# Average pooling over 512 MiB on one core: 4 MiB stores over two tiles, a side buffer for a tile's last sums, and a first load in one piece

## The chip, the cores and the metric

The kernel runs on one core of a Trainium2 chip. The metric is the device time of one execution in microseconds (us). The kernel before takes 1575.64 us, the median of 3 runs between 1575.11 and 1575.70.

The engines that matter here are VectorE (DVE), which adds; ScalarE (ACT), which multiplies and also issues stores; and SyncE (SP), which issues loads and a few stores. Their transfers are carried out by 16 DMA engines, which all three share.

## The reference

```python
x = np.random.randn(64, 256, 8192).astype(np.float32)   # kernel_size = stride = 4
out_len = (length - kernel_size) // stride + 1          # 2048
for i in range(out_len):
    start = i * stride
    output[:, :, i] = np.mean(x[:, :, start : start + kernel_size], axis=2)
```

Each output is the mean of four neighbouring numbers. 536.87 MB are read, 134.22 MB are written, and there is no reuse of anything.

## The kernel before

The input is taken as 16384 rows of 8192 floats, the output as 16384 rows of 2048. A tile is 256 rows: two whole rows (`_R = 2`) for each of the 128 partitions, 64 KiB of input per partition and 8 MiB in all, and 16 KiB of output per partition, 2 MiB in all. There are 64 tiles. A tile is one contiguous piece of HBM, in which a partition's 64 KiB follow directly on the 64 KiB of the partition before (`xg`, line 43).

In SBUF there are two input buffers (`xin`, 2 x 64 KiB per partition) and four output buffers (`res`, 4 x 16 KiB per partition). The order of the work is written out by hand, engine by engine, with semaphores, and no scheduler moves it. Each engine runs a loop over groups of four tiles (`U = _NOUT = 4`), the last group outside it.

- SP (`load`, lines 67 to 74) waits until the sums of the tile two before are done (`s_dve`), and then loads the next tile into that tile's buffer. All loads go through SP's queue. In the last group the last tile is loaded as two halves of one row per partition, each 4 MiB.
- The first tile is loaded by two DMAs (lines 114 and 115): partitions 0 to 15 (`_S = 16`) with the semaphore `s_first`, and partitions 16 to 127 with `s_in[0]`. DVE waits for the first of them at line 130, and for the second in `add_up`.
- DVE (`add_up`, lines 92 to 104) waits until the output buffer has been stored (`s_out`) and the tile has landed (`s_in`). It then adds neighbours twice (`pairs`, line 88): first 16384 floats per partition to 8192, written in place over the front half of the input buffer, then 8192 to 4096, written to the output buffer. Only the second sum gives the input buffer back (`s_dve`).
- ACT (lines 141 to 156) waits for the sums, multiplies the output buffer by 0.25 in place, waits for that, and issues the store of the tile (line 150), 2 MiB. The first tile's store is issued after the second tile's sums (line 142).
- At the end SP issues the stores of tiles 61 and 62 and of the first row of tile 63 behind the last loads (lines 125 to 127), and, after the critical section, the store of the last row, 1 MiB (line 162).

Of the kernel before, what the change touches and what calls it, by code (L numbers as in the profile page):

```python
# [1 line left out]

# [4 lines left out]

_R = 2  # L10

_NIN = 2
_NOUT = 4

_S = 16


@with_exitstack
def kernel(
    ctx: ExitStack,  # L20
    tc: tile.TileContext,
    x: bass.AP,
    kernel_size: bass.AP,
    stride: bass.AP,
    out: bass.AP,
):
    nc = tc.nc
    K = int(kernel_size)
    assert K == int(stride) == 4
    P = nc.NUM_PARTITIONS  # L30
    dt = x.dtype
    inv_k = 1.0 / float(K)

    xf = x.flatten_outer_dims()
    of = out.flatten_outer_dims()
    rows, L = xf.shape
    OL = of.shape[1]
    R = _R
    T, OT = R * L, R * OL
    assert OL * K == L and rows % (P * R * _NOUT) == 0  # L40
    NT = rows // (P * R)

    xg = xf.rearrange("(t p r) m -> p t (r m)", p=P, r=R)
    og = of.rearrange("(t p r) m -> p t (r m)", p=P, r=R)

    pool = ctx.enter_context(tc.tile_pool(name="buf", bufs=1))
    xin = pool.tile([P, _NIN * T], dt)
    res = pool.tile([P, _NOUT * OT], dt)

    s_in = [tc.alloc_semaphore(f"s_in{b}") for b in range(_NIN)]
    s_out = [tc.alloc_semaphore(f"s_out{b}") for b in range(_NOUT)]
    s_dve = tc.alloc_semaphore("s_dve")
    s_act = tc.alloc_semaphore("s_act")
    s_half = tc.alloc_semaphore("s_half")
    s_last = tc.alloc_semaphore("s_last")
    s_first = tc.alloc_semaphore("s_first")

    with tc.tile_critical():  # L60

        U = _NOUT
        E = NT // U - 1

        def load(h, u, r0=0, r1=R, wait=True):
            b = u % _NIN
            if wait:
                nc.sync.wait_ge(s_dve, h * U + (u - _NIN + 1))  # L70
            nc.sync.dma_start(  # L71
                out=xin[:, b * T + r0 * L : b * T + r1 * L],
                in_=xg[:, h * U + u, r0 * L : r1 * L],
            ).then_inc(s_last if r0 > 0 else s_in[b], 16)

        def obuf(u, r0=0, r1=R):
            return res[:, u * OT + r0 * OL : u * OT + r1 * OL]

        def store(eng, h, u, r1=R):

            eng.wait_ge(s_act, h * U + (u + (1 if r1 == R else r1)))
            eng.dma_start(
                out=og[:, h * U + u, : r1 * OL], in_=obuf(u, 0, r1)
            ).then_inc(s_out[u], 16)

        def pairs(out, src):
            v = src.rearrange("p (m k) -> p m k", k=2)
            return nc.vector.tensor_tensor(  # L88
                out=out, in0=v[:, :, 0], in1=v[:, :, 1], op=mybir.AluOpType.add
            )  # L90

        def add_up(h, u, r0=0, r1=R):

            b = u % _NIN
            if r0 > 0:
                nc.vector.wait_ge(s_last, 16)
            else:
                nc.vector.wait_ge(s_out[u], h * 16)
                nc.vector.wait_ge(s_in[b], h * (U // _NIN * 16) + (u // _NIN + 1) * 16)  # L99
            src = xin[:, b * T + r0 * L : b * T + r1 * L]  # L100
            half = src[:, : (r1 - r0) * L // 2]
            pairs(half, src).then_inc(s_half, 1)
            nc.vector.wait_ge(s_half, h * U + (u + 1 + (r0 > 0)))
            pairs(obuf(u, r0, r1), half).then_inc(s_dve, 1)

        def scale(h, u, r0=0, r1=R):
            nc.scalar.wait_ge(s_dve, h * U + (u + 1 + (r0 > 0)))
            o = obuf(u, r0, r1)
            nc.scalar.mul(o, o, inv_k).then_inc(s_act, 1)  # L109

        for p0, p1, sem in ((0, _S, s_first), (_S, P, s_in[0])):
            nc.sync.dma_start(out=xin[p0:p1, :T], in_=xg[p0:p1, 0, :]).then_inc(sem, 16)  # L115
        for u in range(1, _NIN):
            load(0, u, wait=False)
        with nc.sync.Fori(0, E) as h:
            for u in range(_NIN, U + _NIN):
                load(h, u)  # L120
        for u in range(_NIN, U - 1):
            load(E, u)
        for r in range(R):
            load(E, U - 1, r, r + 1, wait=r == 0)
        for u in range(1, U - 1):
            store(nc.sync, E, u)
        store(nc.sync, E, U - 1, R - 1)


        nc.vector.wait_ge(s_first, 16)  # L130
        with nc.vector.Fori(0, E) as h:
            for u in range(U):
                add_up(h, u)
        for u in range(U - 1):
            add_up(E, u)
        for r in range(R):
            add_up(E, U - 1, r, r + 1)

        scale(0, 0)
        nc.scalar.wait_ge(s_dve, 2)
        store(nc.scalar, 0, 0)
        with nc.scalar.Fori(0, E) as h:
            for u in range(1, U + 1):
                v = u % U
                nc.scalar.wait_ge(s_dve, h * U + (u + 1))
                nc.scalar.mul(obuf(v), obuf(v), inv_k).then_inc(s_act, 1)  # L148
                nc.scalar.wait_ge(s_act, h * U + (u + 1))
                nc.scalar.dma_start(out=og[:, h * U + u, :], in_=obuf(v)).then_inc(  # L150
                    s_out[v], 16
                )
        scale(E, 1)
        scale(E, 2)
        scale(E, 3, 0, 1)
        scale(E, 3, 1, 2)

        nc.sync.wait_ge(s_out[0], E * 16 + 16)

    nc.sync.dma_start(
        out=og[:, NT - 1, (R - 1) * OL :], in_=res[:, _NOUT * OT - OL :]
    )


# [1 line left out]
_INS = ['x', 'kernel_size', 'stride']  # L168
_OUTS = [((64, 256, 2048), 'float32')]

_NUMBERS = {'kernel_size': 4, 'stride': 4}


# [26 lines left out]
```

## Time and profile before

| what | value |
|---|---|
| median of 3 runs | 1575.64 us |
| the profiled execution's own time | 1575.64 us |
| its span, first to last instruction | 1573.9 us |
| DVE busy | 839.8 us, 130 instructions |
| ACT busy | 232.9 us, 66 instructions |
| bytes moved by DMA | 671.10 MB, mean 426 GB/s |
| SP's queue (q1) | 543.17 MB, 81.0% of the 16 engines' span |
| ACT's queue (q10) | 127.93 MB, 19.0% |
| DVE's wait for loads | 723.1 us in 65 waits |
| a store of 2 MiB on ACT's queue | 52.8 us from issue to landing, median |

The span leaves out 1.7 us of the profiled execution's own time. The page cuts the span into 40 slices of 39.35 us; for each it gives the busy share of each engine in tenths, of the DMA engines taken together, and the GB/s that they moved. The trace also has a record for every DMA packet (one contiguous run of bytes on one DMA engine) with its start, its duration and its size. A load's packet here is the 64 KiB of one partition, a store's packet the 16 KiB of one partition. The busy share of the DMA engines counts the time that packets took, so a packet that is slow counts as busy too.

### The profile page before, as it was taken

The numbers are of one execution on the slowest core, as the hardware profiler recorded it, in microseconds if no ns is written. First come the engines' busy times: TensorE is split into PE (matmuls) and PEld (weight loads), VectorE is DVE, ScalarE is ACT, GpSimd is POOL, SyncE is SP. The second block draws the span as 40 slices with busy tenths as digits, with TensorE's granted clock in tenths as the row PEclk, the third lists the DMA queues.
The fourth block names the chain that finished last, engine by engine and source line by source line (L and its number), as shares of the span: only waits on it lengthen the run. The fifth ranks groups of instructions, "written<-read, shape, count | busy, mean of one in ns | idle before, by whom it ended". The sixth has DMA issues, their size and how long they took to land.

```text
span 1573.9 us, 977 instructions
## 1 busy us (share of the span) xinstructions
DVE 839.8 (53%) x130; ACT 232.9 (15%) x66; POOL 0.2 (0%) x4
## 2 busy tenths in 40 slices
DVE  0654654645546546456465464564654645646546
ACT  0111111011011111110110111101101111011011
POOL 0000000000000000000000000000000000000000
DMA  9999999999999999999999999999999999999999
GB/s 213 413 428 433 433 433 433 434 433 444 422 436 433 436 434 434 436 434 434 435 433 433 432 434 433 431 437 433 433 433 433 433 433 429 437 433 433 433 428 396
DMA packets 18736, 671.10 MB, mean 426 GB/s; under 512 B 2096, under 2 KB 2096, under 8 KB 2096
## 3 DMA queue, kind: packets, MB, share of 16 engines
q1 hardware_dynamic: 9952, 543.17, 81.0%
q10 hardware_dynamic: 8784, 127.93, 19.0%
HBM read 536.87 MB, written 134.22 MB: 426 GB/s over the span
## 4 chain that ended last, share of the span: by engine, by line
DMA 71%; DVE 27%; another core or an unknown queue 0%; issue 0%; SPq 0%; ACT 0%; DVEq 0%
DMA xin<-in_x_dram 71%; DVE xin L88 18%; DVE res L88 9%; SPq L71 0%; ACT res L109 0%; DVEq L99 0%; SPq L115 0%; SPq L195 0%; SPq L60 0%
## 5 line engine op out<-in xcount | busy, mean ns | idle before, releaser
L88 DVE TENSOR_TENSOR xin<-xin 128x8192 f32<-128x8192 f32 (+1 forms) x65 | 556.5, 8561 | 723.1 <-DMA xin<-in_x_dram 723.1
L148 ACT ACTIVATE res<-res 128x4096 f32<-128x4096 f32 x60 | 217.0, 3616 | 1224.7 <-DVE res L88 1224.7
L88 DVE TENSOR_TENSOR res<-xin 128x4096 f32<-128x4096 f32 (+1 forms) x65 | 283.4, 4359 | 2.2
L109 ACT ACTIVATE res<-res 128x4096 f32<-128x4096 f32 (+1 forms) x5 | 14.7, 2933 | 108.6 <-DVE res L88 108.6
L109 ACT ACT_TABLE_LOAD x1 | 1.3, 1283 | 0.9 <-SPq L60 0.9
L181 POOL MEMSET const-bfloat16-1.0<- 128x1 bf16 x1 | 0.1, 102 | 0.0
L181 POOL MEMSET const-uint8-127<- 128x1 uint8 x1 | 0.1, 102 | 0.0
L181 POOL MEMSET const-float32-1.0<- 128x1 f32 x1 | 0.1, 99 | 0.0
L181 POOL MEMSET const-float32-0.0<- 128x1 f32 x1 | 0.1, 98 | 0.2 <-issue 0.2
## 6 DMA issues: line engine op xcount, KB each, us to landing
out_dram<-res ACTq DMA_DIRECT2D x61, 2048.0 KB, 52.8
xin<-in_x_dram SPq DMA_DIRECT2D x2, 4096.0 KB, 29.5
out_dram<-res SPq DMA_DIRECT2D x2, 2048.0 KB, 26.1
out_dram<-res SPq DMA_DIRECT2D x2, 1024.0 KB, 9.5
xin<-in_x_dram SPq DMA_DIRECT2D x64, 35.0
```

The costliest lines, as they stand in the source:

```text
L88: return nc.vector.tensor_tensor(out=out, in0=v[:, :, 0], in1=v[:, :, 1], op=mybir.AluOpType.add)
L109: nc.scalar.mul(o, o, inv_k).then_inc(s_act, 1)
L148: nc.scalar.mul(obuf(v), obuf(v), inv_k).then_inc(s_act, 1)
L181: nc = _bacc.Bacc("TRN2", target_bir_lowering=False, num_devices=1)
```

## The change

The change has four parts.

1. The first load goes out as one DMA over all 128 partitions, as every other load; `_S`, `s_first` and DVE's wait on it are gone.
2. A group of 512 rows (`_F = 4` rows per partition) makes two tiles, and both results go out as one store of 4 MiB with 32 KiB per partition. The two output buffers hold two tiles each (`_NOUT = 2`, `U = _NOUT * G = 4` tiles per turn of the loop). As a partition now owns four consecutive rows, a tile's load takes 64 KiB of every 128 KiB of HBM.
3. A tile's sums are made in four instructions in place of two. The first 4352 of the first sums go in place and then to the output as before; the last 3840 (`_B`) go to a buffer of their own (`hb`, 15 KiB per partition), and are summed to the output from there. The input buffer is given back after the third instruction by a semaphore of its own (`s_free`), on which the loads wait. The two halves of the last tile are summed as before.
4. The end follows: SP stores tiles 60 and 61 together (4 MiB), then three rows per partition of tiles 62 and 63 (3 MiB), and then the last row (1 MiB), for which it waits on `s_out[1]` in place of `s_out[0]`.

```diff
+_F = 4
-_NOUT = 4
-_S = 16
+_NOUT = 2
+_B = 3840
...
-    xg = xf.rearrange("(t p r) m -> p t (r m)", p=P, r=R)
-    og = of.rearrange("(t p r) m -> p t (r m)", p=P, r=R)
+    og = of.rearrange("(g p f) m -> p g (f m)", p=P, f=F)
+    xg = xf.rearrange("(g p f) m -> p g (f m)", p=P, f=F)
...
-    res = pool.tile([P, _NOUT * OT], dt)
+    res = pool.tile([P, _NOUT * F * OL], dt)
+    hb = pool.tile([P, _B], dt)
...
         def load(h, u, r0=0, r1=R, wait=True):
             b = u % _NIN
             if wait:
-                nc.sync.wait_ge(s_dve, h * U + (u - _NIN + 1))
+                nc.sync.wait_ge(s_free, h * U + (u - _NIN + 1))
             nc.sync.dma_start(
                 out=xin[:, b * T + r0 * L : b * T + r1 * L],
-                in_=xg[:, h * U + u, r0 * L : r1 * L],
+                in_=xg[
+                    :,
+                    h * _NOUT + u // G,
+                    (u % G * R + r0) * L : (u % G * R + r1) * L,
+                ],
             ).then_inc(s_last if r0 > 0 else s_in[b], 16)
...
-        def store(eng, h, u, r1=R):
-            eng.wait_ge(s_act, h * U + (u + (1 if r1 == R else r1)))
+        def store(eng, h, j, scaled, f1=F):
+            eng.wait_ge(s_act, scaled)
             eng.dma_start(
-                out=og[:, h * U + u, : r1 * OL], in_=obuf(u, 0, r1)
-            ).then_inc(s_out[u], 16)
+                out=og[:, h * _NOUT + j, : f1 * OL],
+                in_=res[:, j * F * OL : (j * F + f1) * OL],
+            ).then_inc(s_out[j], 16)
...
+            if u % G == 0 and r0 == 0:
+                nc.vector.wait_ge(s_out[u // G], h * 16)
...
-            half = src[:, : (r1 - r0) * L // 2]
-            pairs(half, src).then_inc(s_half, 1)
+            n = (r1 - r0) * L // 2
+            a = n if r1 - r0 < R else n - _B
+            o = obuf(u, r0, r1)
+            pairs(src[:, :a], src[:, : 2 * a]).then_inc(s_half, 1)
             nc.vector.wait_ge(s_half, h * U + (u + 1 + (r0 > 0)))
-            pairs(obuf(u, r0, r1), half).then_inc(s_dve, 1)
+            last = pairs(o[:, : a // 2], src[:, :a])
+            if a < n:
+                pairs(hb[:, :], src[:, 2 * a :]).then_inc(s_free, 1)
+                nc.vector.wait_ge(s_free, h * U + (u + 1))
+                last = pairs(o[:, a // 2 :], hb[:, :])
+            last.then_inc(s_dve, 1)
...
-        for p0, p1, sem in ((0, _S, s_first), (_S, P, s_in[0])):
-            nc.sync.dma_start(out=xin[p0:p1, :T], in_=xg[p0:p1, 0, :]).then_inc(sem, 16)
-        for u in range(1, _NIN):
+        for u in range(_NIN):
             load(0, u, wait=False)
...
-        for u in range(1, U - 1):
-            store(nc.sync, E, u)
-        store(nc.sync, E, U - 1, R - 1)
-        nc.vector.wait_ge(s_first, 16)
+        store(nc.sync, E, _NOUT - 2, NT - G)
+        store(nc.sync, E, _NOUT - 1, NT - 1 + R - 1, F - 1)
...
-        scale(0, 0)
-        nc.scalar.wait_ge(s_dve, 2)
-        store(nc.scalar, 0, 0)
         with nc.scalar.Fori(0, E) as h:
-            for u in range(1, U + 1):
-                v = u % U
-                nc.scalar.wait_ge(s_dve, h * U + (u + 1))
-                nc.scalar.mul(obuf(v), obuf(v), inv_k).then_inc(s_act, 1)
-                nc.scalar.wait_ge(s_act, h * U + (u + 1))
-                nc.scalar.dma_start(out=og[:, h * U + u, :], in_=obuf(v)).then_inc(
-                    s_out[v], 16
-                )
+            for u in range(U):
+                scale(h, u)
+                if u % G == G - 1:
+                    store(nc.scalar, h, u // G, h * U + (u + 1))
...
-        nc.sync.wait_ge(s_out[0], E * 16 + 16)
+        nc.sync.wait_ge(s_out[_NOUT - 1], E * 16)
```

## Prediction before the change was run

> **What bounds the kernel now.** I read the page's slices first, then the queues, the waits, the chain of waits in order of time, and last the busy time by stretch.
>
> ```profile
> span 1573.9 us, 977 instructions
> ...
> DMA  9999999999999999999999999999999999999999
> GB/s 213 413 428 433 433 433 433 434 433 444 422 436 433 436 434 434 436 434 434 435 433 433 432 434 433 431 437 433 433 433 433 433 433 429 437 433 433 433 428 396
> DMA packets 18736, 671.10 MB, mean 426 GB/s; under 512 B 2096, under 2 KB 2096, under 8 KB 2096
> ```
>
> All 16 DMA engines are busy from the first slice to the last, so this kernel is its transfers. But busy is not the same as moving: the first slice (39 us) moved 213 GB/s, the settled ones 433. In the stretches (columns: stretch, its length, DVE, ACT and POOL busy, granted clock, DMA share, GB/s) the break is sharp:
>
> ```profile
> 0.00:44.85 44.85, 0.00 (x0) 1.28 (x1) 0.20 (x4) 1.00 0.99 222
> 44.85:64.20 19.35, 13.12 (x2) 3.62 (x1) 0.00 (x0) 1.00 1.00 434
> 108.30:156.60 48.30, 26.23 (x4) 7.23 (x2) 0.00 (x0) 1.00 1.00 433
> 156.60:398.30 241.70, 131.18 (x20) 36.16 (x10) 0.00 (x0) 1.00 1.00 434
> ```
>
> Loads alone (44.85 to 64.20) and loads mixed with stores (all later rows) run at the same 434 GB/s. The slow stretch ends with the landing of the first tile, as the chain of waits shows (start, length, what):
>
> ```profile
> 1.40 43.43 DMA xin<-in_x_dram
> 44.85 8.70 DVE xin L88
> 53.58 4.42 DVE res L88
> 58.00 6.16 another core or an unknown queue
> 64.21 0.05 issue
> 64.26 8.71 DVE xin L88
> ```
>
> The first tile is summed from 44.85, the second from 64.26: 19.4 us for 8 MiB, against 43.4 us for the first 8 MiB. The two transfers of the first tile (line 115) show it by themselves, 12.2 us for the 1 MiB of partitions 0 to 15 and 43.4 us for the other 7 MiB, queued behind it:
>
> ```profile
> DMA to landing us min/median/max: 12.2/27.8/43.4
> ```
>
> The compute engines are never late. In the middle of the run DVE idles 11 us before each tile, and the wait is for a load:
>
> ```profile
> 121.63 24.45 SPq L71 DMA_DIRECT2D xin<-in_x_dram  x2
> 125.27 0.34 ACTq L150 DMA_DIRECT2D out_dram<-res  x1
> 132.41 8.69 DVE L88 TENSOR_TENSOR xin<-xin 128x8192 f32<-128x8192 f32 x1 [10.95 <-DMA xin<-in_x_dram]
> 141.13 4.42 DVE L88 TENSOR_TENSOR res<-xin 128x4096 f32<-128x4096 f32 x1
> 145.59 3.62 ACT L148 ACTIVATE res<-res 128x4096 f32<-128x4096 f32 x1 [20.48 <-DVE res L88]
> ```
>
> **What the Trainium skill says.** (1) "SBUF — State Buffer", section "Door 1: The DMA port swizzle": the rate of a DMA depends on how many of 16 SBUF ports its partitions reach. Partitions 0 to 15 reach 4 ports and measured 104 GB/s at 1 MiB; 128 partitions reach all 16. The trace agrees: 1.05 MB landed 12.2 us after its issue, 86 GB/s, and its sixteen 64 KiB packets took 7.5 to 9.3 us each in the packet records of the trace, against 2.418 us of every 64 KiB packet later. (2) "DMA: Bandwidth & Descriptors", "Queues, rings and completion order": each DMA engine takes packets in turn from the queues that have work. The trace agrees: against a 64 KiB load packet a 16 KiB store packet gets a fifth of an engine, so a 2 MiB store needs about a tile period, 24.2 us; with two in flight the page has 52.8 us. (3) The same page, "Latency and other measured facts", on the HBM row pitch: copies of 128 partitions ran at 207 GB/s with a pitch of 512 KiB between partitions where full rate was 214, and at 164 with 2 MiB. The load pitch before is 64 KiB; nothing in its trace shows a larger one.
>
> **The first load goes out whole: the gain.** Before, the packets of the first load start at 1.99 to 2.29 us (packet records), one per engine, and the second tile is complete at 64.10; it lands at 64.19. After, each engine has 8 packets per tile for the first two tiles, all of the same shape as the second load of before. Price: 16 x 2.418 = 38.69 us. From the latest start, 2.29, that is 40.98, and with the same 0.09 us from last packet to landing 41.07. The gain is 64.19 - 41.07 = **23.1 us**, all on the path, since every engine has transfers queued from here to the end. What is late next is simply the second tile, then every load in turn. SP also issues one DMA less (0.40 us) and DVE loses its wait on the small part (line 130); both lie under the first 19 us of transfer and are worth nothing.
>
> **The loops: 4 MiB stores.** A packet takes 2.418 us for 64 KiB, 1.213 for 32 KiB, 0.611 for 16 KiB and 0.309 for 8 KiB in the packet records: a fixed part of 8 to 9 ns above a pure rate. Per tile and engine, 8 store packets of 16 KiB (4.888 us) become 4 of 32 KiB (4.852), 36 ns less; over 64 tiles at most 2.3 us. But the tile period is 24.18 us (from 156.64 to 1462.34 in 54 tiles), and less the 8 load packets (19.344) that leaves 4.836 for the stores, under the 4.888 of their sum: most of the fixed part already overlaps. I count rounds: 8 rounds of load plus store packet and 8 load packets alone per two tiles, with about 10.6 ns of fixed cost per round and 8.6 per packet alone, against 16 rounds before: 16 ns per two tiles, 0.5 us in all. I take **-0.5**, bounds 0 and -2.3.
>
> Could merging starve the loads? A store is issued after the second tile's sums (13.4) and scaling (3.6), 17.4 us after that tile landed, and then takes 8 x (2.418 + 1.206) = 29.0 us, done at 46.4, before the next such store, 48.4 later. It takes a third of the engines for that time, but bytes only change order. The output buffer is wanted again 72.5 us after the landing, cover 26 us; uncovered, it would cost what the store overruns.
>
> **Sums of the last part.** By shape, DVE takes 8.692 us for 8192 outputs, 4.425 for 4096 and 2.292 for 2048: 0.159 us plus 1.0417 ns per output. The new four are 4352, 2176, 3840 and 1920 outputs: 4.69 + 2.43 + 4.16 + 2.16 = 13.44 us against 13.12. So DVE has 0.32 us more per tile, 63 x 0.32 = 20 us in total, under the 11 us of idle time ahead of each tile. Were that cover gone the 20 us would be on the path. The buffer comes free after 11.28 instead of 13.12, 1.84 us sooner. This brings nothing: the load is issued at 121.63 where its predecessor lands at 132.4, so it waits 10.7 us in the queue already. The added waits are DVE on its own third sum, with only its own fourth sum and, later, ACT's scaling queued behind, and ACT's store wait on its own scaling, which is there before too. **0**.
>
> **The end.** SP issues the store of tiles 60 and 61 behind the last loads, then 3 MiB, then 1 MiB. After tile 61 lands, two loads run 38.7 us; the 4 MiB store was issued at 17.4; the 3 MiB one comes at about 41.5, before the 4 MiB is drained at 48.4; the last sum ends at about 46.3, scaling at 48.2, and the last 1 MiB is issued then, while 3 MiB run until about 55.7. No gap. Stores alone take 8 x (1.213 + 0.911 + 0.309) = 19.5 us for the last 8 MiB, against 19.3 had they been mixed: **+0.1**. If a gap did open, the last 1 MiB (2.5 us) is about what it would cost.
>
> **The load pitch.** A tile now takes 64 KiB of every 128 KiB of HBM; pitch 128 KiB instead of 64. Unmeasured here. Bounds: below, nothing to gain, since a 64 KiB packet is at one duration, 2.418 us, in all the settled run; above, the loss that the skill has for 512 KiB, 3.3% of the loads' 512 x 2.418 = 1238 us, 41 us. I take 0, as this pitch is a quarter of the one where the loss is first stated and small.
>
> **Sum.** 1573.9 - 23.1 - 0.5 + 0.1 = 1550.4 for the span. The profiled execution's own time is 1575.64, 1.7 us more than its span and equal to the median; 1550.4 + 1.7 = 1552.1, which I give as **1552**.
>
> **Rivals.** *A: as worked out*, 1552, own range 1550 to 1554 from the bounds of the store packets and the end. *B: the loads get slower by the pitch.* All 16 engines now start within 0.3 us of each other, where the split left them up to 2 us apart (the second tile's packets end between 61.9 and 64.1)[...]. If HBM answers that worse, each 64 KiB packet stretches. It decides from 23.6 / 1238 = 1.9%, a packet of 2.464 us; at 3.3% the time is 1552 + 41 = 1593, slower. For it: no trace shows this start in step. Against: the loads here are paced by the 27 GB/s of one engine to within a nanosecond, which looks like a limit on the chip's side and not HBM's. A little of it, 0.1 to 0.4% of 1238, gives 1553 to 1557. *C: the start is slow by itself*, whatever the partitions (first transfers of a launch), so nothing is won: 1575.6 - 0.4 = 1575. For it: it is the first transfer. Against: the rate changes exactly where the 112 partitions end, and the first part matches four ports. *D: the merged store or the end leaves the engines dry*, a few us each at start and end: 1556 to 1562. Against: the load queue is never empty by more than 8 us of margin, 19.3 less 11.3.
>
> **Chances.** A 0.76, a little of B or D 0.09, C 0.06, B in full 0.09. About 0.2% (3 us) is what a measurement tells from no change. Faster 0.85, within it 0.06, slower 0.09. The range runs from A's lower bound, 1550, to 1557, where the small forms of B end.
>
> **What would show it.** First tile summed from about 21.8 us, second from 41.1; first slice near 410 GB/s instead of 213; tiles 24.17 us apart on average; 4 MiB stores landing after 29 to 31 us; DVE busy 860 us; about 14,100 packets; the last 1 MiB issued 6 or more us before the transfers end. Wrong would be: a first tile at 40 us or more (C), more than 24.3 us between tiles in the middle (B), GB/s under 420 in the last slice but one (D).

## The result and the profile after

| | executions | median us | range us | ratio to before, 95% interval |
|---|---|---|---|---|
| before | 4 | 1575.57 | 1575.11 to 1575.70 | 1 |
| changed, first measured | 4 | 1568.77 | 1565.79 to 1569.61 | 0.9954, 0.9937 to 0.9971 |
| changed, measured again | 11 | 1567.48 | 1554.18 to 1572.21 | 0.9928, 0.9903 to 0.9952 |

The change makes the kernel faster by 0.5 to 0.7%, where 1.5% was forecast. The forecast of 1552 and its range of 1550 to 1557 missed the median. One thing in this table needs a remark: unlike the kernel before, the changed kernel does not take the same time in each execution, and two of its fifteen took 1554.18 and 1554.35 us, inside the forecast range.

The page of the changed kernel, from an execution of 1568.01 us:

```profile
span 1566.2 us, 991 instructions
...
DMA  9999999999999999999999999999999999999998
GB/s 423 407 449 435 428 426 440 426 439 428 428 422 435 428 428 425 426 430 431 428 427 427 439 433 428 425 437 423 432 428 437 430 423 441 427 432 417 439 425 384
DMA packets 14112, 671.09 MB, mean 428 GB/s; under 512 B 1568, under 2 KB 1568, under 8 KB 1568
```

The first slice moved 423 GB/s instead of 213, so the slow start is gone. But the slices in the middle, most of which stood at 433 to 434 before, now vary between 417 and 449. Taken over longer windows (start and end, length, DVE, ACT and POOL busy, clock, DMA share, GB/s):

```profile
0.00:44.85 44.85, 16.07 (x5) 4.90 (x2) 0.20 (x4) 1.00 0.99 421
...
110.00:400.00 290.00, 160.14 (x48) 45.48 (x14) 0.00 (x0) 1.00 1.00 433
400.00:800.00 400.00, 218.30 (x66) 64.75 (x22) 0.00 (x0) 1.00 1.00 428
800.00:1200.00 400.00, 222.08 (x67) 64.51 (x21) 0.00 (x0) 1.00 1.00 431
1200.00:1500.00 300.00, 160.14 (x48) 48.05 (x15) 0.00 (x0) 1.00 1.00 429
```

The DMA share is still 1.00, so the engines are not without work; they move fewer bytes while busy. The chain of waits (start, length, what) shows the start nearly as forecast, and then tiles too far apart:

```profile
0.95 21.83 DMA xin<-in_x_dram
22.80 4.70 DVE xin L99
...
61.47 4.70 DVE xin L99
...
1526.71 4.70 DVE xin L99
```

The first tile is summed from 22.80 us, where it was 44.85. From the third tile (61.47) to the 63rd (1526.71) there are 60 tiles, 24.42 us each, against 24.18 before. 0.24 us on 64 tiles is 15 us. The issues (count, KB each, us to landing) show a store that is done long before the next one, 48.8 us later:

```profile
out_dram<-res ACTq DMA_DIRECT2D x30, 4096.0 KB, 33.4
```

The packet records of the trace say where the 0.24 us are. Most packets still take exactly what they took before: 2.418 us for 64 KiB, 1.213 for 32 KiB. But after the first 90 us 618 of 11,904 packets take longer, nearly all of them 64 KiB load packets and most of them around the start of a 4 MiB store, up to 3.6 us. The records don't name the engine, but a packet starts within a few ns of the end of the one before it on its engine, and so the packets can be put in chains. This is the store issued at 156.99 us, for six of the 16 engines (starts of packets in us after the issue, "+" the ns over 2418; S marks a store packet, the others are load packets):

```
-1.25  1.16         3.58+98  S6.09  7.30+169  S9.88
-1.26  1.16         3.57     S5.99  7.19+369  S9.98
-0.99  1.43  S3.84  5.05+129 S7.60  8.81+89
-0.90  1.52  S3.93  5.14+417 S7.97  9.18
-0.75  1.67  S4.09  5.30     S7.71  8.92+306
-1.26  1.17  S3.58  4.79     S7.21  8.41+89
```

And this, for three engines, is the first store of all, issued at 59.35 us, where all 16 engines show it:

```
-1.16  1.27  3.69+901  S7.00
-0.88  1.56  3.97+891  S7.28
-1.10  1.33  3.74+934  S7.09
```

From here on a **stretch** is what a packet takes beyond the usual time of its size (counted from 25 ns up); given is the sum over all packets divided by the 16 engines. The changed kernel has 14.1 us of it, 12.4 us after the first 90 us: 0.43 us on average for the 29 stores that ACT issues there, from 0.02 to 0.77. Of the 12.4 us, 3.7 fall on the load packet just ahead of an engine's first store packet, 4.4 on the one between the first and the second store packet, 1.7 on the next, and 1.6 on the last two that alternate with the store. The kernel before has no stretch after its first load.

### The profile page after: what moved, and what is told of

It is laid out like the page before. It is cut to its first block, busy times and chain, and to the rows that moved or that the text cites. A ratio compares the mean times of both kernels' runs of the same rounds, so it can differ in the third digit from the quotient of the medians.

```text
span 1566.2 us, 991 instructions
## 1 busy us (share of the span) xinstructions
DVE 854.0 (55%) x256; ACT 250.9 (16%) x80; POOL 0.2 (0%) x4
## 2 busy tenths in 40 slices
DMA packets 14112, 671.09 MB, mean 428 GB/s; under 512 B 1568, under 2 KB 1568, under 8 KB 1568
## 4 chain that ended last, share of the span: by engine, by line
DMA 75%; DVE 24%; issue 0%; SPq 0%; ACT 0%; DVEq 0%
DMA xin<-in_x_dram 75%; DVE xin L99 10%; DVE hb L99 8%; DVE res L99 5%; SPq L81 0%; ACT res L132 0%; DVEq L115 0%; SPq L205 0%; SPq L69 0%
## 5 line engine op out<-in xcount | busy, mean ns | idle before, releaser
L99 DVE TENSOR_TENSOR xin<-xin 128x4352 f32<-128x4352 f32 (+1 forms) x65 | 304.5, 4684 | 695.1 <-DMA xin<-in_x_dram 695.1
L132 ACT ACTIVATE res<-res 128x4096 f32<-128x4096 f32 (+1 forms) x65 | 231.6, 3564 | 1291.7 <-DVE res L99 1291.7
L99 DVE TENSOR_TENSOR hb<-xin 128x3840 f32<-128x3840 f32 x63 | 261.6, 4152 | 0.0
L99 DVE TENSOR_TENSOR res<-xin 128x2176 f32<-128x2176 f32 (+1 forms) x65 | 157.4, 2421 | 2.2
L99 DVE TENSOR_TENSOR res<-hb 128x1920 f32<-128x1920 f32 x63 | 135.9, 2158 | 2.2
## 6 DMA issues: line engine op xcount, KB each, us to landing
out_dram<-res ACTq DMA_DIRECT2D x30, 4096.0 KB, 33.4
```

The source lines that it names most:

```text
L99: return nc.vector.tensor_tensor(out=out, in0=v[:, :, 0], in1=v[:, :, 1], op=mybir.AluOpType.add)
```

## The experiments

Every kernel below is measured beside the kernel before, in 4 executions (the changed kernel again in 11). "Stretch" is that after the first 90 us, in the profiled execution. The edits show the lines that matter; what follows from them, as semaphore counts and the last tiles, is left out. Theories were numbered as they came up: 1, the store queue runs empty before each store; 2, the 16 engines start in step, since the first load is not split; 3, the HBM pitch of the loads; 4, the 32 KiB store packets; 5, an empty store queue together with 64 KiB load packets.

### The first load whole, and nothing else

```diff
-        for p0, p1, sem in ((0, _S, s_first), (_S, P, s_in[0])):
-            nc.sync.dma_start(out=xin[p0:p1, :T], in_=xg[p0:p1, 0, :]).then_inc(sem, 16)
-        for u in range(1, _NIN):
+        for u in range(_NIN):
             load(0, u, wait=False)
...
-        nc.vector.wait_ge(s_first, 16)
```

> The kernel before with one edit: the first load goes out as one DMA over 128 partitions. Theory 1 (the slow load packets of the changed kernel come each time the store queue goes from empty to busy; here two stores are always queued, so it never does): 23 us less than before, 1552 to 1553 us, and no 64 KiB packet over 2.44 us after the first sixteen. Theory 2 (they come because the 16 DMA engines start in step; the split first load put them out of step): slow packets here too, 1560 to 1570 us. Theory 3 (they come from the 128 KiB load pitch): 1552 to 1553 us, as theory 1.

Measured: 1554.91 us, ratio 0.9869 (0.9853 to 0.9886), stretch 0. The whole gain of the start is there, and the middle runs as before:

```profile
0.00:44.85 44.85, 15.75 (x3) 4.90 (x2) 0.20 (x4) 1.00 0.99 421
...
400.00:800.00 400.00, 221.34 (x34) 57.86 (x16) 0.00 (x0) 1.00 1.00 434
800.00:1200.00 400.00, 211.88 (x34) 61.48 (x17) 0.00 (x0) 1.00 1.01 435
```

Theory 2 falls: the engines start in step here too. The 2 to 3 us above the expectation stand at two places in the main, 0.77 us in the first 16 packets after the launch and 0.98 us in the load packet ahead of the very first store.

### The changed kernel with the first load split again

```diff
-        for u in range(_NIN):
+        for p0, p1, sem in ((0, _S, s_first), (_S, P, s_in[0])):
+            nc.sync.dma_start(
+                out=xin[p0:p1, :T], in_=xg[p0:p1, 0, :T]
+            ).then_inc(sem, 16)
+        for u in range(1, _NIN):
             load(0, u, wait=False)
...
+        nc.vector.wait_ge(s_first, 16)
         with nc.vector.Fori(0, E) as h:
```

> The changed kernel with the first load split again into 16 and 112 partitions. Theory 1 and theory 3: slow load packets stay, about 14 us of them per engine, and the 22 us of the slow start come on top: 1588 to 1592 us. Theory 2: the engines are out of step, no slow packets, 1574 to 1577 us.

Measured: 1587.20 us (1584.21 to 1595.07), ratio 1.0067 (1.0051 to 1.0084), stretch 18.8 us in the execution of 1595.07. The split costs 18 to 20 us beside the two medians of the changed kernel and cures nothing: theory 2 falls again. It also shows the rest of the change by itself, since only the start is as before: the other three parts together make the kernel slower, by 0.7%.

### Only the layout

```diff
-    xg = xf.rearrange("(t p r) m -> p t (r m)", p=P, r=R)
-    og = of.rearrange("(t p r) m -> p t (r m)", p=P, r=R)
+    xg = xf.rearrange("(g p f) m -> p g (f m)", p=P, f=2 * R)
+    og = of.rearrange("(g p f) m -> p g (f m)", p=P, f=2 * R)
...
-                in_=xg[:, h * U + u, r0 * L : r1 * L],
+                in_=xg[:, h * 2 + u // 2, u % 2 * T + r0 * L : u % 2 * T + r1 * L],
```

on the kernel with the first load whole, the stores likewise.

> The kernel before with the first load whole and only the layout of the changed kernel: a tile takes 64 KiB of every 128 KiB of input, and its 2 MiB store 16 KiB of every 32 KiB of output; one store per tile, two of them always queued. Theory 1: 1552 to 1553 us, no slow packets. Theory 2: as the run with the whole first load alone. Theory 3: slow packets, 1560 to 1570 us.

Measured: 1554.90 us, ratio 0.9869 (0.9852 to 0.9885), stretch 0, to 0.01 us the time without it. Theory 3, the forecast's rival B, falls: a pitch of 128 KiB instead of 64 costs nothing here.

### The changed kernel with all stores in SP's queue

```diff
             for u in range(_NIN, U + _NIN):
                 load(h, u)
+                v = u - _NIN
+                if v % G == G - 1:
+                    store(nc.sync, h, v // G, h * U + (v + 1))
...
                 scale(h, u)
-                if u % G == G - 1:
-                    store(nc.scalar, h, u // G, h * U + (u + 1))
```

> The changed kernel with its 4 MiB stores issued by SP behind the loads, so that there is only one queue and it is never empty. Theory 1: no slow load packets, 1550 to 1553 us. Theory 2 and theory 3: the engines still start in step and the pitch is the same, so slow packets stay, 1562 to 1570 us.

Measured: 1557.96 us (1557.77 to 1558.26), ratio 0.9888 (0.9871 to 0.9904), stretch 1.7 us. The same 4 MiB stores with the same packets lose 10 us of their stretch when they stand in the loads' own queue. It is 5 us over the expectation. 3.3 us are stretches over the whole run (1.8 in the kernel with only the first load whole); another part is the end, where some engines have no packet left while others work: 2.8 us per engine on average in the last 12 us, against 0.3 in the kernel with only the first load whole.

### One store at a time, and smaller load packets

First, the store of the first tile is no longer held back to keep two in the queue (on the kernel with the first load whole):

```diff
         scale(0, 0)
-        nc.scalar.wait_ge(s_dve, 2)
         store(nc.scalar, 0, 0)
```

> The kernel before with the first load whole and the first tile's store issued at once in place of after the second tile's sums, so that only one 2 MiB store is queued at a time. Theory 1: a store needs 24.2 us at a fifth of the engines and the next one is issued 24.2 us later, but it needs 3.4 us or more from issue to its first packet, so the queue runs empty before each store and the load packet ahead of each first store packet is stretched: 62 stores at 0.2 to 0.45 us, 1567 to 1583 us. Rival (the stretch comes from the 32 KiB store packets or the 4 MiB stores, not from an empty queue): 1555 us, as with the hold.

Measured: 1554.53 us (1554.18 to 1554.56), ratio 0.9866 (0.9849 to 0.9882), stretch 0. Neither side is decided by it, as the queue did not run empty after all: a store lands 31.5 us after its issue, more than the 24.2 to the next one, and in the packet records 6.8 us of its packets are left when the next is issued.

```profile
out_dram<-res ACTq DMA_DIRECT2D x61, 2048.0 KB, 31.5
```

So the queue was emptied by force. Load packets of 32 KiB leave a 16 KiB store packet a third of an engine instead of a fifth:

```diff
-            nc.sync.dma_start(
-                out=xin[:, b * T + r0 * L : b * T + r1 * L],
-                in_=xg[:, h * U + u, r0 * L : r1 * L],
-            ).then_inc(s_last if r0 > 0 else s_in[b], 16)
+            for r in range(r0, r1):
+                nc.sync.dma_start(
+                    out=xin[:, b * T + r * L : b * T + (r + 1) * L],
+                    in_=xg[:, h * U + u, r * L : (r + 1) * L],
+                ).then_inc(s_last if r0 > 0 else s_in[b], 16)
```

> The kernel before with the first load whole and each 8 MiB load issued as two of 4 MiB, one row per partition each, so that a load packet is 32 KiB; stores as before, 2 MiB in 16 KiB packets. A store now gets a third of the engines and is done after about 15 us, so the queue is empty before each store, 62 times. The smaller packets cost by themselves about 8 x 8 ns per tile, 4 us. Theory 1: 62 stretched load packets of 0.2 to 0.45 us per engine on top: 1571 to 1587 us. Rival (32 KiB store packets or 4 MiB stores are to blame): 1555 to 1560 us.

The second of this pair issues two stores together after every second tile:

```diff
         with nc.scalar.Fori(0, E) as h:
-            for u in range(1, U + 1):
...
+            for u in range(U):
+                scale(h, u)
+                if u % 2:
+                    store(nc.scalar, h, u - 1)
+                    store(nc.scalar, h, u)
```

> As the run with 32 KiB load packets, but the two stores of a pair of tiles are issued one behind the other after the second tile's scaling: the same packets and bytes, and the store queue goes from empty to busy 31 times in place of 62. Theory 1: half the excess of that run over its 1559 us without stretches: 1565 to 1573 us. Rival: the same time as that run within 2 us.

Measured: 1559.07 us (ratio 0.9895, 0.9879 to 0.9912) and 1559.50 us (0.9898, 0.9881 to 0.9914), stretch 0 in both. The first one's stores (count, KB each, us to landing):

```profile
out_dram<-res ACTq DMA_DIRECT2D x61, 2048.0 KB, 18.5
```

18.5 us to landing at one store per 24 us: the queue is empty before each. The rival was right, and **theory 1 falls in its simple form**: an emptied queue by itself stretches nothing. The smaller load packets cost the 4 us that their number let expect.

### The changed kernel without the side buffer

```diff
-                nc.sync.wait_ge(s_free, h * U + (u - _NIN + 1))
+                nc.sync.wait_ge(s_dve, h * U + (u - _NIN + 1))
...
-            a = n if r1 - r0 < R else n - _B
+            a = n
```

> The changed kernel without the side buffer: two sums per tile as before, and the input buffer given back after the second, 1.84 us later. Both theories: the same time as the changed kernel within its own spread, 1566 to 1570 us, since the load is issued about 10 us before its predecessor lands. If the early give-back is what brings the store's start and the load's into collision, it is 3 us or more faster.

Measured: 1554.36, 1580.24, 1583.20 and 1586.59 us; the profile is that of 1580.24, with a stretch of 24.1 us, 14.3 us of it on the load packet just ahead of an engine's first store packet. No ratio can be given for four times so far apart. The stretches do not need the side buffer, and this kernel too has an execution without the loss. Three of the four lie above all fifteen executions of the changed kernel (at most 1572.21 us), so the side buffer seems to have made the stretches smaller (12 to 15 us with it). Four executions do not show by how much, nor why.

### Packet size or empty queue

The next three kernels and the changed one again ran on one chip. The changed kernel with 32 KiB load packets (the edit of above, in its `load`):

> The changed kernel with each 8 MiB load issued as two of 4 MiB, so that a load packet is 32 KiB beside store packets of 32 KiB; the queue of stores is empty most of the time. The smaller packets cost some 4 us. Theory 4 (a 32 KiB store packet behind an empty queue stretches the load packet ahead of it, whatever the load packet's size): stretches stay, 1563 to 1573 us. Theory 5 (the stretch needs 64 KiB load packets and an empty store queue): 1554 to 1560 us.

Measured: 1562.76 us (1561.70 to 1570.16), ratio 0.9934 (0.9909 to 0.9959), stretch 1.4 us in the execution of 1561.70 that was profiled. Unlike the two kernels with 32 KiB load and 16 KiB store packets, all within 0.6 us of 1559, it varies by 8 us. Its median lies between the two expectations, and its executions of 1563.66 and 1570.16 us have no profile.

Next, on the kernel with the first load whole, stores of even tiles in SP's queue and of odd tiles in ACT's:

```diff
                 load(h, u)
+                if u % 2 == 0:
+                    store(nc.sync, h, u - _NIN)
...
+            for u in range(U):
+                scale(h, u)
+                if u % 2:
+                    store(nc.scalar, h, u)
```

> The kernel before with the first load whole, and the 2 MiB stores of even tiles issued by SP behind the loads, those of odd tiles by ACT. Load packets 64 KiB, store packets 16 KiB; ACT's queue holds 24 us of work per 48 us, so it is empty before each of its 31 stores. Theory 4: no stretched packets but at the first store, 1553 to 1557 us. Theory 5: 31 stretches of about 0.45 us per engine, 1565 to 1572 us.

Measured: 1557.28 us (1556.58 to 1557.55), ratio 0.9883 (0.9866 to 0.9899), stretch 0.5 us. The time is 0.3 us above the range of theory 4, and the stretch is far from the 14 us of theory 5.

```profile
out_dram<-res ACTq DMA_DIRECT2D x30, 2048.0 KB, 22.7
```

ACT's queue holds 22.7 us of work in each 48 us, the load packets are 64 KiB, and the starts of 16 KiB stores stretch next to nothing. **Theory 5 falls.** Half of the stores went to SP's queue in this kernel, though.

The next one issues one 4 MiB store per two tiles, all from ACT up to the last four tiles, but of 16 KiB packets:

```diff
+        def store2(eng, h, j):
+            eng.wait_ge(s_act, h * U + (2 * j + 2))
+            eng.dma_start(
+                out=og2[:, h * 2 + j],
+                in_=res[:, 2 * j * OT : (2 * j + 2) * OT].rearrange(
+                    "p (t m) -> p t m", t=2
+                ),
+            ).then_inc(s_out[2 * j + 1], 16)
```

> The kernel before with the first load whole and one 4 MiB store per two tiles, as two runs of 16 KiB per partition: merged as in the changed kernel, but with 16 KiB packets, which get a fifth of the engines, so that the store fills nearly the whole 48 us to the next. Theory 4 and theory 5: no or few stretches, 1553 to 1558 us. If it is the 4 MiB store as such, of any packets: 1565 to 1572 us.

Measured: 1555.07 us, ratio 0.9869 (0.9853 to 0.9886), stretch 0. It is not the size of the store.

```profile
out_dram<-res ACTq DMA_DIRECT2D x30, 4096.0 KB, 49.5
```

It decides more than was planned. A store lands 49.5 us after its issue and the next is issued after 48.4, so the queue looks filled; but the landing comes later than the last packet. In the packet records, at 22 of the 29 next issues, the last store packet had ended 0.4 to 1.6 us before, and the next store's first packet came 4.3 to 5.6 us after that end. So this queue runs empty too, beside 64 KiB load packets, and nothing is stretched: theory 5 falls a second time, though here the queue is empty for far shorter than in the changed kernel (17.6 us before the next issue).

> The changed kernel once more beside these, on one chip: 1565 to 1570 us if its stretches come the same way in every execution; a value near 1553 among them would show that the stretches depend on how the engines happen to fall in step.

Measured: 1554.18, 1554.35, 1559.48, 1562.18, 1565.07 and six between 1567.48 and 1572.21 us. Stretch 14.6 us in a profiled execution of 1570.29, 6.5 of it on the load packet just ahead of an engine's first store packet and 5.8 on the one between the first and the second. The second sign came, two values at 1554: the stretches differ from execution to execution. That it is how the engines fall in step is not shown; no execution near 1554 has a profile.

### The 32 KiB packets undone, and the 32 KiB packets with a filled queue

```diff
-            eng.dma_start(
-                out=og[:, h * _NOUT + j, : f1 * OL],
-                in_=res[:, j * F * OL : (j * F + f1) * OL],
-            ).then_inc(s_out[j], 16)
+            for f in range(0, f1, R):
+                f2 = min(f + R, f1)
+                eng.dma_start(
+                    out=og[:, h * _NOUT + j, f * OL : f2 * OL],
+                    in_=res[:, (j * F + f) * OL : (j * F + f2) * OL],
+                ).then_inc(s_out[j], 16)
```

> The changed kernel with each 4 MiB store issued as two DMAs of 2 MiB one behind the other, two rows per partition each, so that its store packets are 16 KiB; all else as changed (side buffer, layout, one point of issue per two tiles). If the 32 KiB store packets bring the stretches: 1554 to 1556 us in every execution. If it is anything else that the change brought along: 1554 to 1572 us, as the changed kernel.

Measured: 1555.05 us (1554.65 to 1555.62), ratio 0.9868 (0.9852 to 0.9885), stretch 0. In the middle of the run (columns as above) it moves what the kernel before moved:

```profile
400.00:800.00 400.00, 222.93 (x67) 62.99 (x20) 0.00 (x0) 1.00 1.00 433
800.00:1200.00 400.00, 218.52 (x67) 66.60 (x21) 0.00 (x0) 1.00 1.00 433
...
out_dram<-res ACTq DMA_DIRECT2D x60, 2048.0 KB, 43.5
```

By their times, all four executions lost their stretches by this one edit. It changes two things at once, though: 16 KiB packets take a fifth of an engine, so the two stores fill the queue for the whole 48 us (43.5 us to landing, the median of first and second). The last kernel parts them the other way, with 32 KiB packets in a queue that stays filled. In the changed kernel it loads and sums only every second tile, and writes each result twice, so that half of the reference's output is missing:

```diff
-            for u in range(_NIN, U + _NIN):
+            for u in range(_NIN, _NOUT + _NIN):
                 load(h, u)
...
+            nc.scalar.mul(obuf(u * G + 1), obuf(u * G), inv_k).then_inc(s_act, 1)
+            nc.scalar.mul(obuf(u * G), obuf(u * G), inv_k).then_inc(s_act, 1)
```

> The changed kernel with the loads and the sums of every second tile left out (ACT writes the even tile's result a second time in its place): one 8 MiB load of 64 KiB packets per 4 MiB store of 32 KiB packets, 29 us of transfers for each, so that the next store is issued before the last one is through and the store queue stays filled. By bytes about 935 us. If 32 KiB packets stretch load packets only where the store queue was empty: no stretches after the first stores. If they do in any case, whenever a store begins: 31 stretches of about 0.45 us per engine, 14 us in all.

Measured: 948.50 us (948.17 to 948.85), stretch 0.1 us. The 13 us over the estimate from the bytes are the end: between 920 and 940 us the engines have no packet for 13.1 us on average. The middle runs at full rate:

```profile
100.00:400.00 300.00, 137.63 (x41) 77.63 (x25) 0.00 (x0) 1.00 1.00 433
400.00:800.00 400.00, 182.63 (x56) 108.68 (x35) 0.00 (x0) 1.00 1.00 434
...
out_dram<-res ACTq DMA_DIRECT2D x30, 4096.0 KB, 37.2
```

A store lands 37.2 us after its issue, and the next is issued after 29 (300.49, 329.55 and 358.50 us in the timeline), when 5.3 us or more of packets are left of the one before: the queue is filled, and 32 KiB store packets beside 64 KiB load packets stretch nothing.

Together:

| store packets | store queue | load packets | stretch, us |
|---|---|---|---|
| 32 KiB | own, runs empty | 64 KiB | 12.4, 14.6, 18.8, 24.1 (changed, again, first load split, no side buffer) |
| 32 KiB | own, runs empty | 32 KiB | 1.4, times vary by 8 us |
| 32 KiB | the loads' own | 64 KiB | 1.7 |
| 32 KiB | own, filled | 64 KiB | 0.1 (half of the loads left out) |
| 16 KiB | own, runs empty | 64 KiB | 0.5 (every second store), 0 (4 MiB stores, empty for 0.4 to 1.6 us before most issues) |
| 16 KiB | own, runs empty | 32 KiB | 0, 0 |
| 16 KiB | own, filled | 64 KiB | 0 in the kernel before and four others |

The stretches came where a store of 32 KiB packets began in a queue of its own that had run empty, and hardly anywhere else. Theory 4 stands only with that addition: neither the packets alone nor the empty queue alone brings the loss. The two conditions go together in the change: store packets of half the size of the load packets with which they alternate take a third of the engine, and this empties the queue. The filled 32 KiB queue rests on one kernel with half the loads, so it differs from the changed kernel in more than the queue.

What happens inside a DMA engine at that moment, and why two executions in fifteen are, by their times, free of it, stays open. The records show that a stretched packet can end before the engine's first store packet starts, or lie between two store packets, and nothing of what the engine fetches meanwhile.

Five of these kernels come to about 1555 us, below the medians of both the kernel before and the changed one, and stay within 1 us from execution to execution: the kernel before with the first load whole (1554.91 us), the same without the hold (1554.53), with the layout (1554.90), with merged stores of 16 KiB packets (1555.07), and the changed kernel with 16 KiB store packets (1555.05). They have in common the whole first load, which brings 20.7 us by itself, and store packets of 16 KiB beside load packets of 64.

## Why the prediction was wrong

**The start: right in mechanism, too large in size.** The second tile's sums were forecast to move by 23.1 us, from 64.26 to about 41.1. They came at 42.12 in the changed kernel and at 42.22 in the kernel where only the first load was changed. 0.75 us of the difference are in the first 16 packets, which took 3.17 us on average instead of 2.418. The time of the kernel with only this edit fell by 20.7 us. The forecast compared the latest engine before (64.10 us) with the latest after; but averaged over the engines, the packets of the first load were stretched by 21.2 us, and 1.75 us of stretches came anew, at the first packets and the first store. A more even end gave back 1.4 us. Rival C falls: the start was slow because of the split, which brought 18 to 20 us back when it was restored. Ports as the cause of the split's price, taken from the Trainium skill ("SBUF — State Buffer", "Door 1: The DMA port swizzle"), fits the 16 partitions, which by that section reach four of 16 ports, but was not varied by itself. It leaves most of the price open. By the same section the other 112 partitions reach all 16 ports; yet their packets took 4.63 us (median) and not the 2.418 that the prediction gave to every later packet, and they make up 15.0 of the 21.2 us.

**The step that failed: the 4 MiB stores.** The prediction put the merged store at -0.5 us with bounds of 0 and -2.3, from the durations of packets, and held that "bytes only change order". The packets of the store were indeed as priced, 1.213 us for 32 KiB, and the count of all packets, 14,112, was right. What was left out is what the start of such a store does to the load packets around it. The trace of before has 61 stores of ACT but its queue never runs empty after the first, and no store packets of 32 KiB, so it could not show it. An unseen case was priced at nothing, with an upper bound of nothing, although the same text worked out that a store is through 29 us after its issue and the next comes after 48.4, so that the queue is empty in between. Measured in its place: 0.43 us on average for each store, 12.4 us in the profiled execution, up to 24 in a relative of the kernel. A store landed 33.4 us after its issue, where 29 to 31 were forecast.

**The sum.** 1550.4 us were forecast for the span, 1566.2 measured, 15.8 more. 14.1 us are the stretches, of which 0.75 and 0.92 us fall on the first packets and the first store. 1.9 us are the difference of 23.1 and 21.2 at the start. The end is less even: in the last 12 us of transfers an engine has no packet for 2.4 us on average, against 1.6 before, and the last packets of the engines end between 1560.0 and 1565.0 us. Against this, the fewer packets save about 1.4 us in place of 0.5, an estimate from their durations and the 4 ns by which one overlaps the next on its engine. Together this comes to about the 15.8 us.

**The rivals.** The spacing of 24.42 us in the middle is the sign that was named for rival B, but B's cause is ruled out: neither the pitch nor the start in step costs anything after the first 90 us. Rival D had the right part, the merged store, and the wrong mechanism: between the first 5 and the last 12 us the engines have no packet for 0.8 us on average, the same as in the kernel before.

**Right:** DVE's longer work (854.0 us) is hidden, and the end has no gap: the last 1 MiB was issued at 1555.5 us, 9.5 us before the transfers ended. That the early give-back of the input buffer is worth 0 is not confirmed: the kernel without it had the larger stretches.

## What to carry to other kernels

When transfers are the bound, price not only packets and bytes but also what a transfer does to others as it starts; if the trace of before has no such start, the bound of its cost is not zero. Here a start in an empty queue was as good as free with store packets of 16 KiB (0 to 0.5 us in a whole run), and packets of 32 KiB in a filled queue were too (0.1 us); both together cost 12 to 24 us. Larger store packets are not free of risk: they take a bigger share of each engine, drain their queue sooner and so start anew in an empty one. Stores in 16 KiB packets beside loads in 64 KiB, the same 1 to 4 as the bytes, took nearly the whole time to the next store and kept the packets at their constant time.

## What the hardware showed that was not expected

- Away from the stretches, a DMA packet takes the same time to a nanosecond over a whole run: 7631 of 7634 load packets of 64 KiB took 2.418 us after the first 90 us in the kernel before, and 7496 of 7536 where 128 instead of 64 KiB lie between partitions in HBM.
- The first packets after the launch (0.5 to 0.8 us) and those around the first stores (0.6 to 1.4 us, between 10 and 90 us) are stretched in every kernel with the whole first load, also where no stretch comes later. In the two with the split first load the first store brings none.
- The same program with the same data took between 1554.18 and 1572.21 us, where its relatives with 16 KiB store packets and a filled queue stay within 1 us.
- ACT loads its table 15 times in the changed kernel, 1.28 us each, about once per turn of its loop; before it did so once. In these runs every kernel with an ACTIVATE ahead of the loop has one load, and every one without has 15. It lies in ACT's idle time: with 15 loads a kernel still takes 1555.05 us.
